# Four kinds of tiles at other places modulo 512 bytes, and the third group's values of two head pairs as one product of 512 columns

## The chip, the cores and the metric

The kernel runs on one core of a Trainium2 chip. The metric is device time in microseconds of one execution; less is better. A core has a matrix engine (TensorE, PE in the profile; its loading of the operand that stays in the array is listed apart as PEld), VectorE (DVE), ScalarE (ACT), GpSimd (POOL) and SyncE (SP, which issues DMAs here). They run side by side and wait for each other through semaphores; each works through its own instructions in the order in which the program has them.

## The reference

Four residual layers over x of 256 tokens by 1024 features, `x = x + mixer(rms_norm(x))`, with the mixers A, B, C, A. Each mixer is one input projection that also makes a gate z, some mixing, a product with silu(z), and an output projection.

```python
def mixer_a(h, w_in, v_gain, w_s, b_s, w_out):      # layers 0 and 3
    u, v, z = split(h @ w_in)                       # 2048 columns each
    mixed = einsum('gij,bcjgd->bcigd', tril(w_s), rms_norm(v, v_gain)) + b_s
    return (u * mixed * silu(z)) @ w_out

def mixer_b(h, w_in, q_gain, k_gain, w_out):        # layer 1: 8 heads of 128, three groups g
    for g, (window, dilation) in enumerate(((128, 1), (512, 4), (2048, 16))):
        q, k = rotary(rms_norm(q_g)), rotary(rms_norm(k_g))
        o_g, lse_g = banded_softmax_attention(q, k, v_g)
    return (sum_g softmax(lse)_g * o_g * silu(z)) @ w_out

def mixer_c(h, w_in, w_grp, scale, w_out):          # layer 2: four pooling groups g
    mixed_g = (causal_mean(x_g, window_g) - x_g) @ w_grp[g]
    return (mixed * scale * silu(z)) @ w_out
```

## The kernel before

**Products.** Every fp32 number that enters a large product is split in two tiles, an upper half (name ending in h, written by ScalarE, `hi_of`, line 85) and the remainder (ending in l, written by VectorE, `lo_of`, line 88). `mm3` (lines 80 to 82) then makes a product of three matrix instructions: upper by upper, upper by lower, lower by upper. In `mm3(out, lh, rh)` the tile lh is loaded into the array and rh streams past; the profile prints the streaming one first where names are told apart.

**Weights** come as 272 units of 128 by 1024 (`wts`, made on the host by `_weight_stream`). SP loads a unit into a raw tile wr (4 buffers); ScalarE and VectorE make w<n>h and w<n>l of it (7 pairs). `step` keeps that work a few units ahead of the product: the order in which these halves stand between an engine's other instructions is fixed when the program is built.

**Order.** The program is written by one Python loop that emits the projections. Side work stands in generators (`spawn`), and each `tick`, one per half unit of products, lets those that are due emit their next piece. `need(key)` ticks until a side task has emitted what the next product reads. So all five engines' orders are fixed, and how much work of TensorE stands between two steps of a side chain (its cover) comes from how many ticks lie between them.

**Projections.** `proj_tok` makes a product by tokens: h^T is loaded (tile hT, layout 128 by 8 by 256 per half) and 512 columns of weights stream; a unit takes 12 instructions. `proj_feat` makes it by features: weights are loaded and 256 columns of h^T stream; a unit takes 24. Both use PSUM banks of the tag pp (4 banks). Mixing uses the tag at (3 banks).

**Layer 1** (`layer_b`) runs over four head pairs hp of two heads. Of each it makes q and k of the three groups (qk, 4 units each), the values of the first two groups (v01, 4 units, 512 columns) and the values of the third (v2p, lines 1010 to 1019: 2 units, 256 columns). The gate (bz, two `proj_feat`) stands after the first qk. Side chains: `qk_task` (norm, rotation, transposes qt), `score_task` for each of two heads (scores s, maximum with the mask, exp into p, division by the sum), and `mix_task` (lines 909 to 976): five chunks, each of transposes pt of p, halves pT<hp><chunk>h and l, and products onto the tile o. A step of its loop emits the transposes of chunk i, the lower half of chunk i-1 and the products of chunk i-2. Then `gated` multiplies o with the gate (szT) and makes the halves yb<hp>. `proj_out` follows: units w144 to w147 for the first two pairs, w148 and w149 for the third (yb2), w150 and w151 for the fourth (yb3); the last four run for tokens 0 to 127 and then again for 128 to 255.

**Places.** hT holds two halves and 16 spare columns, and `h_parts` (line 267) shifts its start by 64 bytes in some layers. Odd widths of small tiles (32 in place of 16 for csc, line 1034) move the tiles behind them.

Of the kernel before, what the change touches and what calls it, by code (L numbers as in the profile page):

```python
# [10 lines left out]
F32 = mybir.dt.float32  # L11
# [6 lines left out]
P = 128  # L18
# [32 lines left out]
def hybrid_trunk_kernel(ctx, tc, x, wts, norm_gainT, a_v_gain, a_wsT, a_bsT, b_gl, b_gv, c_scaleT,  # L51
# [7 lines left out]
    dp = ctx.enter_context(tc.tile_pool(name="dp", bufs=1, space=bass.MemoryType.DRAM))  # L59

# [23 lines left out]
    def hi_of(hi, src):  # L84
        nc.scalar.activation(hi, src, AF.Copy)
# [66 lines left out]
    last_pool = [None]  # L152
# [10 lines left out]
    def load_units(n):  # L163
        while loaded[0] < min(n, n_seq):
            i = loaded[0]
            tag = raw_place(i)
            pool = {"wr": wp, "xs": cp, "wx": last_pool[0]}[tag]
            raw = pool.tile([P, 2, HALF], F32, tag=tag, name=f"wr{i}", bufs=len(raw_users[tag]))
            raw_users[tag] = raw_users[tag][1:] + [i]
            src = sums[seq[i][0], seq[i][2]][seq[i][1]] if isinstance(seq[i], tuple) else wts[seq[i]]  # L170
            nc.sync.dma_start(raw, src.rearrange("p (k n) -> p k n", n=HALF))
            raws.append(raw)
            loaded[0] += 1

    def sums_of_quarters(parts):
# [3 lines left out]
        for n, j, c in parts:  # L179
            z = seven_units(n) + j  # L180
            cs = slice(c * 256, (c + 1) * 256)
            q = cp.tile([P, 4, 256], F32, tag="xs", name=f"qs{n}{j}{c}", bufs=1)
# [84 lines left out]
    def h_parts(layer):  # L267

        o = 16 if layer in (0, DEPTH - 1) else 0
        return [hT[:, o + i * KT * S:o + (i + 1) * KT * S].rearrange("p (k s) -> p k s", s=S) for i in range(2)]  # L270
# [271 lines left out]
    def layer_a(layer, consts, pl, mid):  # L542
        hcur[:] = h_parts(layer)
        last_pool[0] = pl
# [10 lines left out]
        def v_task(n, o):  # L555
# [31 lines left out]
            for t in range(2):  # L587
                yield 1
                wh, wl = pair(pl, [P, 8, P], "wsr", f"wsr{layer}{t}", 2)
# [194 lines left out]
    def layer_b(layer, consts, pl):  # L784
# [124 lines left out]
        def mix_task(hp, vals, szT):  # L909
            vh, vl, v2h, v2l = vals  # L910

            def val(g, t, h):
# [3 lines left out]
                sl = slice(h * HD, (h + 1) * HD)  # L916
# [44 lines left out]
            for i in range(nch + 2):  # L961
                if i >= 2:
                    while ("v", hp) not in done or ("v2", hp) not in done:
                        yield 1
                    product(i - 2)
# [12 lines left out]
        def val_task(hp, o, vh, vl):  # L978
# [5 lines left out]
            done.add(("v", hp))  # L984

        def val2_task(hp, vp, v2h, v2l):
            fl = "p t c -> p (t c)"
            hi_of(v2h.rearrange(fl), vp)
            yield 1
            lo_of(v2l.rearrange(fl), vp, v2h.rearrange(fl))  # L990
            done.add(("v2", hp))
# [8 lines left out]
        for hp in range(NHEAD // 2):  # L1000
# [6 lines left out]
            o = proj_tok(f"v01{hp}")  # L1007
            vh, vl = pair(pl, [P, 2, HALF], "v01", f"v01{hp}", 1)
            spawn(val_task(hp, o, vh, vl))
            vp = pp(f"v2p{hp}")  # L1010
            for j in range(2):
                w = [a.rearrange("p a b -> p (a b)") for a in next_unit()]
                for kk in range(4):
                    k = 4 * j + kk
                    ws = [a[:, kk * 256:(kk + 1) * 256] for a in w]
                    for t in range(2):
                        mm3(vp[:, t * 256:(t + 1) * 256], h_t(k, t), ws, k == 0 and t == 0, k == KT - 1)
                    if kk % 2:
                        step(kk // 2)
            v2h, v2l = pair(pl, [P, 2, 256], "v2", f"v2{hp}", 1)  # L1020
            spawn(val2_task(hp, vp, v2h, v2l))
# [10 lines left out]
    def layer_c(layer, pl):  # L1032
        hcur[:] = h_parts(layer)
        csc = pl.tile([P, 32], F32, name="csc")[:, :16]
# [83 lines left out]
        def group_task(g, o):  # L1118
            yh, yl = pair(pl, [P, 4, S], "cy", f"cy{g}", 4)
# [82 lines left out]
def _weight_stream(a_w_in, a_w_out, b_w_in, b_w_out, c_w_in, c_w_grp, c_w_out):  # L1202
# [13 lines left out]
    for hp in range(4):  # L1216
        def cols(kind, g):
            c = kind * 3072 + g * 1024 + hp * 256
            return w[:, c:c + 256]
# [6 lines left out]
        parts.append(cols(2, 2).reshape(2, 4, P, 256).transpose(0, 2, 1, 3).reshape(2, P, UNIT))  # L1226
# [86 lines left out]
```

## Time and profile before

| | us |
|---|---|
| median of three runs | 836.82 (833.32, 837.32, 836.82) |
| the profiled execution, whole | 833.59 |
| its span, first to last instruction | 831.8 |
| stretch of layer 0 / 1 / 2 / 3 in it | 0 to 189 / 189 to 491 / 491 to 620 / 620 to 831.8 |

How such a profile is read. The page gives busy time by engine and the chain of work that ended last, followed back from the end. The list of waits says who waited for whom. The timeline has one instruction in a row: its start in us from the span's start, its duration in us, the engine, the line of the source, the operation, output and inputs by name, the shape, and in square brackets the engine's idle time before it with what ended it. Instructions of TensorE are pipelined: a product of 512 columns is shown with 0.39 us, but the next one starts 0.23 us later. What one more product costs is therefore read from the distance of two starts, not from the duration.

### The profile page before, as it was taken

How to read it: one execution, taken by the hardware profiler on the slowest of the kernel's cores; microseconds unless marked ns; L12 is line 12 of the kernel's file. 1: busy time of each engine (PE TensorE's matmuls, PEld its weight loads, DVE VectorE, ACT ScalarE, POOL GpSimd, SP SyncE). 2: the span in 40 equal slices, each digit the busy share in tenths (PEclk: the TensorE clock that was granted, in tenths of full speed). 3: DMA queues.
4: the chain of work that ended last, by engine and by line, in shares of the span. 5: the costliest groups of instructions: out<-in, count | busy, mean ns of one | idle time of the engine just before them, and what ended most of it. 6: DMA issues, size and time to landing. Idle time of an engine off the chain costs nothing.

```text
span 831.8 us, 12513 instructions
## 1 busy us (share of the span) xinstructions
PE 825.4 (99%) x4565; PEld 713.8 (86%) x4565; DVE 590.5 (71%) x1006; ACT 507.3 (61%) x937; POOL 42.6 (5%) x69
## 2 busy tenths in 40 slices
PE   8999999999999999999999999999999999999998
PEld 7888888888988888888888889999978888888886
DVE  4777657646857678678678577798864798787951
ACT  6765454336768687688688567446553667555740
POOL 0201000000000010010010012000000000000000
PEclk9999999999999999999999999999999999999999
DMA  7878666652867546556555268767675377685831
GB/s 272 284 262 276 236 204 203 217 191 82 260 237 229 176 145 236 178 168 212 178 156 199 77 212 277 236 194 230 235 264 180 102 261 240 200 327 167 323 127 51
DMA packets 60654, 172.66 MB, mean 208 GB/s; under 512 B 5584, under 2 KB 22496, under 8 KB 60464
## 3 DMA queue, kind: packets, MB, share of 16 engines
q1 hardware_dynamic: 59328, 167.79, 60.7%
q0 software_dynamic: 976, 3.79, 1.5%
q8 instruction: 36, 0.59, 0.3%
q10 hardware_dynamic: 288, 0.28, 0.1%
q14 instruction: 26, 0.21, 0.1%
HBM read 162.40 MB, written 9.44 MB: 207 GB/s over the span
## 4 chain that ended last, share of the span: by engine, by line
PE 89%; DVE 5%; DMA 3%; issue 1%; ACT 1%; SPq 0%; ACTq 0%; DVEq 0%
PE wo L80 6%; PE wo L82 6%; PE wo L81 6%; PE qk L82 5%; PE qk L80 5%; PE qk L81 5%; PE v L80 5%; PE v L82 5%; PE v L81 5%; PE z L82 3%; PE z L80 3%; PE u L80 3%; PE u L81 3%; PE z L81 3%; PE u L82 3%; PE qt L832 1%
## 5 line engine op out<-in xcount | busy, mean ns | idle before, releaser
L807 POOL TENSOR_TENSOR qr<-qm,m 128x8 f32<-128x8 f32 x12 | 19.9, 1660 | 228.3 <-DVE qm L806 228.3
L802 ACT ACTIVATE junk<-qk 128x128 bf16<-128x128 f32 x96 | 26.7, 278 | 7.3 <-PE qk L82 4.6
L811 ACT ACTIVATE qn<-qk,qr 128x128 f32<-128x128 f32 x96 | 27.6, 382 | 3.5 <-POOL qr L807 3.5
L186 DVE TENSOR_TENSOR qs<-qs 128x256 f32<-128x256 f32 x64 | 26.9, 420 | 3.8 <-DMA qs<-in_wts_dram 3.3
L512 DVE TENSOR_TENSOR x<-wo,x 128x512 f32<-128x512 f32 x16 | 11.0, 690 | 20.1 <-PE wo L82 20.0
L308 ACT ACTIVATE hT<-hp,gT 128x128 fp32r<-128x128 f32 x48 | 13.1, 383 | 14.9 <-PE hp L304 14.9
L806 DVE TENSOR_SCALAR qm<-qs 128x8 f32<-128x8 f32 x12 | 2.1, 172 | 23.7 <-ACT junk L802 23.7
L802 ACT ACTIVATION_READ_ACCUMULATOR junk<-qk 128x1 f32 x96 | 18.8, 196 | 0.0
L313 DVE SCALAR_TENSOR_TENSOR hT<-hp,gT,hT 128x128 fp32r<-128x128 f32 x48 | 13.5, 344 | 7.4 <-ACT hT L308 7.4
L290 POOL TENSOR_TENSOR r<-ms,m 128x1 f32<-128x1 f32 x6 | 4.3, 710 | 273.6 <-DVE ms L287 273.6
L282 ACT ACTIVATE junk<-x 128x512 bf16<-128x512 f32 x16 | 10.2, 640 | 9.6 <-DVE x L512 9.4
L901 ACT ACTIVATE p<-p,rl 128x384 f32<-128x384 f32 (+1 forms) x16 | 11.5, 769 | 5.0 <-DVE rl L900 5.0
L624 DVE SCALAR_TENSOR_TENSOR sz<-u,m,sz 128x512 f32<-128x512 f32 x8 | 6.0, 746 | 12.1 <-PE u L82 12.1
L832 PE MATMUL qt<-ident,qn 128*128 128x128 f32 x96 | 14.4, 273 | 0.1
L832 PEld LDWEIGHTS qt<-ident,qn 128*128 128x128 f32 x96 | 11.5, 140 | 3.0 <-issue 0.7
L824 DVE TENSOR_TENSOR rb<-qn,kcb 128x32 f32<-128x32 f32 x96 | 13.8, 184 | 0.0
L562 DVE TENSOR_TENSOR vv<-v,kc 128x512 f32<-128x512 f32 x16 | 10.7, 687 | 4.1 <-ACT junk L560 3.7
L897 ACT ACTIVATE p<-p,nb 128x768 f32<-128x768 f32 x8 | 7.5, 938 | 7.3 <-DVE nb L896 7.3
L820 DVE TENSOR_TENSOR ra<-qn,kcb 128x64 f32<-128x64 f32 x48 | 10.6, 221 | 0.8 <-ACT qn L811 0.2
L629 DVE SCALAR_TENSOR_TENSOR yy<-mx,bs,sz 128x256 f32<-128x256 f32 x24 | 10.5, 480 | 0.4
L391 DVE SCALAR_TENSOR_TENSOR hT<-hp,gT,hT 128x256 fp32r<-128x256 f32 x8 | 3.5, 476 | 9.4 <-ACT hT L387 9.4
L932 PE MATMUL pt<-ident,p 128*128 128x128 f32 x48 | 9.9, 274 | 0.0
(2887 smaller groups left out, 3314.3 us busy)
## 6 DMA issues: line engine op xcount, KB each, us to landing
wr<-in_wts_dram SPq DMA_DIRECT2D x267, 512.0 KB, 4.3
qs<-in_wts_dram SPq DMA_DIRECT2D x16, 512.0 KB, 5.0
sums<-qs SPq DMA_DIRECT2D x16, 512.0 KB, 6.2
wr<-sums SPq DMA_DIRECT2D x16, 512.0 KB, 4.4
kc<-in_a_wsT_dram POOLq DMA_DIRECT2D x2, 512.0 KB, 7.2
kc<-in_a_v_gain_dram POOLq DMA_DIRECT2D x1, 1024.0 KB, 5.0
out_dram<-x SPq DMA_DIRECT2D x4, 256.0 KB, 2.0
kc<-in_a_v_gain_dram POOLq DMA_DIRECT2D x1, 768.0 KB, 6.0
```

What stands on the lines that cost most here:

```text
L80: nc.tensor.matmul(out_ap, lh[0], rh[0], start=start, stop=False, skip_group_check=True)
L81: nc.tensor.matmul(out_ap, lh[0], rh[1], start=False, stop=False, skip_group_check=True)
L82: nc.tensor.matmul(out_ap, lh[1], rh[0], start=False, stop=stop, skip_group_check=True)
L186: nc.vector.tensor_tensor(q[:, a], q[:, a], q[:, b], op=ALU.add)
L308: nc.scalar.activation(h_parts(layer)[0][:, k, t * P:(t + 1) * P], pt[:, k % 4], AF.Copy, scale=gT[:, layer, k:k + 1])
L313: nc.vector.scalar_tensor_tensor(hTl, pt[:, k % 4], gT[:, layer, k:k + 1], hTh.bitcast(F32), op0=ALU.mult, op1=ALU.subtract)
L802: nc.scalar.activation(junk[:, :HD], ov[t][:, h], AF.Square, accum_out=ssq[t][:, h:h + 1])
L807: nc.gpsimd.tensor_tensor(rqs, ms, m05_row[:, :8], op=ALU.pow)
L811: nc.scalar.activation(qn[t][:, h], ov[t][:, h], AF.Copy, scale=rq[t][:, h:h + 1])
L824: nc.vector.tensor_tensor(rb[:, hs, s0:s0 + 16], qn[t][:, hs, s1:s1 + 16], c, op=ALU.mult)
L832: nc.tensor.transpose(pts[t][:, h], qn[t][:, h], ident)
L901: nc.scalar.activation(f, f, AF.Copy, scale=rl[i][:, 0:1])
```

## The change

Five tiles or groups of tiles start at other places. The places follow from the sizes of the tiles allocated before them; as the built programs lay them out, modulo 512 bytes:

| tile | role in the product | before | after |
|---|---|---|---|
| w..h, w..l (weights) | streams or is loaded | 384 | 384 |
| hT in layers 0 and 3 | loaded | 384 | 384 |
| hT in layer 1 | loaded in qk, v01, v2; streams in bz | 320 | 384 |
| hT in layer 2 | streams in cx, cz; loaded in the first cz | 320 | 320 |
| cd (differences, product cg of layer 2) | streams | 256 | 320 |
| wsr (w_s rows times the norm, product mx) | loaded | 384 | 192 |
| v01 (values, product o) | loaded | 384 | 192 |
| v2 (third group's values, product o) | loaded | 384 | 384 |
| cy (layer 2's y, product wo) | loaded | 384 | 128 |
| pT, qk, yb, v and y of layers 0 and 3 | either | 384 | 384 |

The third group's values are made for two head pairs at once, after the even pair's v01: `proj_tok` with 512 columns, 4 units; the odd pairs make none. The host orders their weights so, and the units keep their number. The upper half of these values goes to the tile xs of the pool cp, which the norms use too. The tiles stage (for the quarter sums of layer 3's weights, which shared xs before) and wx (a raw weight tile of layer 3's) now are tiles of their own from the start. The scratch for the descriptors of the DMAs that POOL issues is 8192 bytes in place of 16384.

```diff
+    stage = cp.tile([P, 4, 256], F32, name="stage")
+    wx = cp.tile([P, 2, HALF], F32, name="wx")
...
-            pool = {"wr": wp, "xs": cp, "wx": last_pool[0]}[tag]
-            raw = pool.tile([P, 2, HALF], F32, tag=tag, name=f"wr{i}", bufs=len(raw_users[tag]))
+            raw = wx if tag == "wx" else (wp if tag == "wr" else cp).tile(
+                [P, 2, HALF], F32, tag=tag, name=f"wr{i}", bufs=len(raw_users[tag]))
...
-            q = cp.tile([P, 4, 256], F32, tag="xs", name=f"qs{n}{j}{c}", bufs=1)
+            q = stage
...
-        o = 16 if layer in (0, DEPTH - 1) else 0
+        o = 0 if layer == 2 else 16
...
+                if t == 0:
+                    pl.tile([P, 80], F32, name="gap")
                 wh, wl = pair(pl, [P, 8, P], "wsr", f"wsr{layer}{t}", 2)
...
-                sl = slice(h * HD, (h + 1) * HD)
+                sl = slice(hp % 2 * 256 + h * HD, hp % 2 * 256 + (h + 1) * HD)
                 return v2h[:, t, sl], v2l[:, t, sl]
...
-                    while ("v", hp) not in done or ("v2", hp) not in done:
+                    while ("v", hp) not in done or ("v2", hp - hp % 2) not in done:
...
             o = proj_tok(f"v01{hp}")
+            if hp == 0:
+                pl.tile([P, 80], F32, name="gap1")
             vh, vl = pair(pl, [P, 2, HALF], "v01", f"v01{hp}", 1)
-            spawn(val_task(hp, o, vh, vl))
-            vp = pp(f"v2p{hp}")
-            for j in range(2):
...
-                        mm3(vp[:, t * 256:(t + 1) * 256], h_t(k, t), ws, k == 0 and t == 0, k == KT - 1)
...
-            v2h, v2l = pair(pl, [P, 2, 256], "v2", f"v2{hp}", 1)
-            spawn(val2_task(hp, vp, v2h, v2l))
+            if hp == 0:
+                pl.tile([P, 48], F32, name="gap2")
+            spawn(val_task(("v", hp), o, vh, vl))
+            if hp % 2 == 0:
+
+                v2h = cp.tile([P, 2, HALF], F32R, tag="xs", name=f"v2{hp}h", bufs=1)
+                v2l = pl.tile([P, 2, HALF], F32R, tag="v2l", name=f"v2{hp}l", bufs=1)
+                spawn(val_task(("v2", hp), proj_tok(f"v2{hp}"), v2h, v2l))
             spawn(mix_task(hp, (vh, vl, v2h, v2l), szT[:, hp]), LAST_LAG if hp == NHEAD // 2 - 1 else MIX_LAG)
...
-        csc = pl.tile([P, 32], F32, name="csc")[:, :16]
+        csc = pl.tile([P, 48], F32, name="csc")[:, :16]
...
+            if not yT:
+                pl.tile([P, 48], F32, name="gap")
             yh, yl = pair(pl, [P, 4, S], "cy", f"cy{g}", 4)
...
-        parts.append(cols(2, 2).reshape(2, 4, P, 256).transpose(0, 2, 1, 3).reshape(2, P, UNIT))
+        if hp % 2 == 0:
+            parts.append(_units(np.concatenate([cols(2, 2), cols(2, 2, 1)], axis=1)))
...
-    nc = _bacc.Bacc("TRN2", target_bir_lowering=False, num_devices=1)
+    nc = _bacc.Bacc("TRN2", target_bir_lowering=False, num_devices=1,
+                     dynamic_dma_scratch_size=8192)
```

How the engines' orders move, at three places. TensorE at the first head pair's values, where v01's last product ends; before, the third group's values of this pair alone (v2p, 256 columns):

```order
L80 MATMUL v_1_2361<-w87h,hT 128x512
L81 MATMUL v_1_2361<-w87l,hT 128x512
L82 MATMUL v_1_2361<-w87h,hT 128x512
L80 MATMUL v2p_2487<-w88h,hT 128x256
L81 MATMUL v2p_2487<-w88l,hT 128x256
L82 MATMUL v2p_2487<-w88h,hT 128x256
```

and after, where v_0_2487 is the third group's product for two pairs:

```order
L84 MATMUL v_1_2358<-w87h,hT 128x512
L85 MATMUL v_1_2358<-w87l,hT 128x512
L86 MATMUL v_1_2358<-w87h,hT 128x512
L84 MATMUL v_0_2487<-w88h,hT 128x512
L85 MATMUL v_0_2487<-w88l,hT 128x512
L86 MATMUL v_0_2487<-w88h,hT 128x512
```

The product of 512 columns has moved in from the second pair. Next, TensorE at the end of layer 1, in the last pair's mixing: o is the mixing's output, pt the transposes of the probabilities p, wo the output projection. Before:

```order
L82 MATMUL o_4845<-pT30h,v013l 128x256
L932 MATMUL pt_4921<-ident,p_4754 128x128
L930 MATMUL pt_4921<-ident,p_4823 128x128
L932 MATMUL pt_4921<-ident,p_4824 128x128 x2
L80 MATMUL wo_00_4809<-w146h,yb1h 128x512
L81 MATMUL wo_00_4809<-w146l,yb1h 128x512
L82 MATMUL wo_00_4809<-w146h,yb1l 128x512
L80 MATMUL wo_10_4811<-w146h,yb1h 128x512
L81 MATMUL wo_10_4811<-w146l,yb1h 128x512
L82 MATMUL wo_10_4811<-w146h,yb1l 128x512
L80 MATMUL o_4845<-pT31h,v23h 128x256
```

and after:

```order
L86 MATMUL o_4676<-pT30h,v013l 128x256
L936 MATMUL pt_4864<-ident,p_4694 128x128
L934 MATMUL pt_4864<-ident,p_4744 128x128
L936 MATMUL pt_4864<-ident,p_4745 128x128 x2
L84 MATMUL o_4676<-pT31h,v22h 128x256
L85 MATMUL o_4676<-pT31l,v22h 128x256
L86 MATMUL o_4676<-pT31h,v22l 128x256
```

The half unit of wo between the third transposes and the products on pT31 now stands earlier, beside the scores; the two later chunks have lost theirs too. Last, VectorE at the same end: w<n>l are weights' lower halves, rl the reciprocals of the second head's sums, szT the gating. Before:

```order
L88 TENSOR_TENSOR pT30l<-pt_4882,pT30h 128x512
L900 RECIPROCAL rl_4832<-l_4830 128x1
L900 RECIPROCAL rl_4833<-l_4831 128x1
L88 TENSOR_TENSOR pT31l<-pt_4896,pT31h 128x512
L88 TENSOR_TENSOR pT32l<-pt_4921,pT32h 128x512
L88 TENSOR_TENSOR w149l<-wr_4666,w149h 128x1024
L88 TENSOR_TENSOR pT33l<-pt_4948,pT33h 128x512
```

and after:

```order
L900 TENSOR_SCALAR nb_4750<-mx_4748 128x1
L92 TENSOR_TENSOR w150l<-wr_4597,w150h 128x1024
L92 TENSOR_TENSOR w151l<-wr_4624,w151h 128x1024
L92 TENSOR_TENSOR pT30l<-pt_4814,pT30h 128x512
L904 RECIPROCAL rl_4753<-l_4751 128x1
L904 RECIPROCAL rl_4754<-l_4752 128x1
L92 TENSOR_TENSOR pT31l<-pt_4839,pT31h 128x512
L92 TENSOR_TENSOR pT32l<-pt_4864,pT32h 128x512
```

The lower halves of the last two output units, which stood behind the first gating, now stand ahead of pT30l and the reciprocals.

More of the change, by code (lines that the diff above doesn't have):

```diff
@@ L151, in hybrid_trunk_kernel @@
     raw_users = {"wr": [-1] * RAW_BUFS, "xs": [-1], "wx": [-1]}
-    last_pool = [None]
     def raw_place(i):
@@ L543, in layer_a @@
         hcur[:] = h_parts(layer)
-        last_pool[0] = pl
         first = proj_first(f"v{layer}0") if layer == 0 else None
@@ L976, in mix_task, with val_task @@
             done.add(("yb", hp))
-        def val_task(hp, o, vh, vl):
+        def val_task(key, o, vh, vl):
             for t in range(2):
@@ L983, in val_task @@
                 lo_of(vl[:, t], o[t], vh[:, t])
[L984 to L991, printed above, removed]
+            done.add(key)
         def gate(b):
@@ L1007, in layer_b @@
             o = proj_tok(f"v01{hp}")
+            if hp == 0:
+                pl.tile([P, 80], F32, name="gap1")
             vh, vl = pair(pl, [P, 2, HALF], "v01", f"v01{hp}", 1)
-            spawn(val_task(hp, o, vh, vl))
-            vp = pp(f"v2p{hp}")
-            for j in range(2):
[L1012 to L1016, printed above, removed]
-                        mm3(vp[:, t * 256:(t + 1) * 256], h_t(k, t), ws, k == 0 and t == 0, k == KT - 1)
-                    if kk % 2:
-                        step(kk // 2)
-            v2h, v2l = pair(pl, [P, 2, 256], "v2", f"v2{hp}", 1)
-            spawn(val2_task(hp, vp, v2h, v2l))
+            if hp == 0:
[5 more added lines that the diff above has]
+                spawn(val_task(("v2", hp), proj_tok(f"v2{hp}"), v2h, v2l))
             spawn(mix_task(hp, (vh, vl, v2h, v2l), szT[:, hp]), LAST_LAG if hp == NHEAD // 2 - 1 else MIX_LAG)
@@ L1216, in _weight_stream, with cols @@
     for hp in range(4):
-        def cols(kind, g):
-            c = kind * 3072 + g * 1024 + hp * 256
+        def cols(kind, g, after=0):
+            c = kind * 3072 + g * 1024 + (hp + after) * 256
             return w[:, c:c + 256]
```

## The prediction

> **What bounds the kernel now.** I read the page first, for the share of each engine and the chain that ended last.
>
> ```profile
> span 831.8 us, 12513 instructions
> ...
> PE 825.4 (99%) x4565; PEld 713.8 (86%) x4565; DVE 590.5 (71%) x1006; ACT 507.3 (61%) x937; POOL 42.6 (5%) x69
> ...
> PE 89%; DVE 5%; DMA 3%; issue 1%; ACT 1%; SPq 0%; ACTq 0%; DVEq 0%
> ```
>
> TensorE is busy for 99% of the span and carries 89% of the chain. The second view is the list of TensorE's waits, which is complete with three rows:
>
> ```profile
> PE warm L276 <- POOL m L258: 1.4, 1, 1.4
> PE hp L380 <- DMA x<-in_x_dram: 0.8, 2, 0.5
> PE wo L80 <- DVE cyy L1126: 0.2, 1, 0.2
> ```
>
> All its waits that the view lists come to 2.4 us, and 2.2 of them lie before the first product. So a change can win only by making TensorE's own stream shorter, and it can lose by giving TensorE something to wait for. A busy PE is modelled, so the third view is the timeline: the distance between the *starts* of products, which I call the pitch, tells what a product really costs.
>
> **Places and pitch.** The rows below are starts, each the first of a weight unit or a run; the count between two rows is the program's. "Place" is a tile's start modulo 512 bytes, from the table ahead.
>
> ```profile
> 526.23 0.28 PE L80 MATMUL cx<-hT,w164h 128*128 128x256 f32 x1
> ...
> 528.95 0.28 PE L80 MATMUL cx<-hT,w165h 128*128 128x256 f32 x1
> ...
> 567.45 0.28 PE L80 MATMUL cg<-cd2h,w179h 128*128 128x256 f32 x1
> ...
> 570.30 0.28 PE L80 MATMUL cx<-hT,w180h 128*128 128x256 f32 x1
> ...
> 70.21 0.28 PE L80 MATMUL mx<-v00h,wsr00h 128*128 128x256 f32 x1
> ...
> 71.64 0.40 PE L80 MATMUL u<-w22h,hT 128*128 128x512 f32 x1
> ...
> 209.67 0.28 PE L80 MATMUL bz<-hT,w69h 128*128 128x256 f32 x1
> ...
> 212.39 0.28 PE L80 MATMUL bz<-hT,w70h 128*128 128x256 f32 x1
> ...
> 470.19 0.28 PE L80 MATMUL o<-pT30h,v013h 128*128 128x256 f32 x1
> ...
> 470.90 0.27 PE L932 MATMUL pt<-ident,p 128*128 128x128 f32 x1
> ```
>
> - cx: 24 products of 256 columns in 2.72 us, 113.3 ns each. Moving operand h^T at 320, weights loaded at 384. bz, the gate of the second layer, stands the same way and has the same 113.3.
> - cg: 24 in 2.85 us, 118.75 ns. The same shape and the same weights, but the moving differences stand at 256.
> - mx: 12 in 1.43 us, 119.2 ns; both operands at 384. o: 6 in 0.71 us, 118.3 ns; both at 384.
>
> So a 256 column product is 5 to 6 ns dearer in three of the four pairs of places that occur, and only 320 against 384 is free. For 512 columns:
>
> ```profile
> 43.01 0.39 PE L80 MATMUL v<-w12h,hT 128*128 128x512 f32 x1
> ...
> 45.73 0.39 PE L80 MATMUL v<-w13h,hT 128*128 128x512 f32 x1
> ...
> 434.41 0.39 PE L80 MATMUL qk<-w136h,hT 128*128 128x512 f32 x1
> ...
> 437.16 0.39 PE L80 MATMUL qk<-w137h,hT 128*128 128x512 f32 x1
> ```
>
> In the first layer, with h^T (here the loaded operand) at 384, 12 products take 2.72 us, 226.7 ns each; in the second, with h^T at 320, 2.75 us, 229.2 ns.
>
> The Trainium skill speaks against all of this: its page "SBUF — State Buffer", section "SBUF: two separate sides", says that only the port pair shared by VectorE and GpSimd contends and that "PE, ACT, and DVE's dedicated pair never wait on anyone". By that rule the places cost nothing, and the sum would be +1.7 (rival 2) where the rows give -1.7; cx and cg, 113.3 and 118.75 with the same shape, disagree with it.
>
> **The change, part by part.**
>
> *h^T of the second layer from 320 to 384.* 576 products of qk and 192 of v01 load it. 768 x 2.5 ns = **-1.9 us**. The same move makes bz (192 products, h^T moving) a 384 against 384 pair, as mx is: 192 x (119.2 - 113.3) = **+1.1 us**. Both classes occur in the trace, so I take them whole; the ends are -1.2 for the first, if only part of the rows have the extra, and 0 for the second.
>
> *cg's differences from 256 to 320.* 192 products become the free pair: 192 x 5.45 ns = **-1.05 us**.
>
> *w_s rows and v01 from 384 to 192; the third layer's y (cy) from 384 to 128.* The trace has none of these pairs. For 256 columns the ends are 113.3 and 119.2; I take 113.3, because 192 lies 256 bytes, half a turn, from a distance of 448, the only one that is free. mx: 96 x 5.9 = **-0.57 us**, and 48 of o's 256 column products, 48 x 5 = **-0.2 us**. For cy, 190 products of 512 columns, the ends are 0 and 190 x 2.5 = +0.5; I take 0, since 128 lies half a turn from 384.
>
> *Third group's values.* Four times 48 products of 256 columns become two times 48 of 512.
>
> ```profile
> 452.25 0.28 PE L80 MATMUL v2p<-w142h,hT 128*128 128x256 f32 x1
> ...
> 453.67 0.60 PE L832 MATMUL qt<-ident,qn 128*128 128x128 f32 x4
> ...
> 455.47 0.28 PE L80 MATMUL v2p<-w143h,hT 128*128 128x256 f32 x1
> ...
> 456.83 0.22 PE L80 MATMUL s<-qk30h 128*128 128x128 f32 x1
> 456.89 0.28 PE L81 MATMUL s<-qk30l,qk30h 128*128 128x128 f32 x1
> ...
> 457.78 0.33 PE L80 MATMUL v2p<-w143h,hT 128*128 128x256 f32 x1
> ```
>
> One run of 12 has 1.42 us (118.3 ns), another 1.36 (113.3). 96 new ones at 226.7 are 21.8 us; 192 old ones are 21.8 to 22.7. I take 118 for most: **-0.8 us**, ends 0 and -0.95. Units, VectorE and ScalarE halves and evacuations stay as many.
>
> *What the move takes away: cover.* The last head pair no longer has its 48 v2p products (5.6 us) between its v01 and the output product. In the new order the output product's units w144 to w147 run while scores are made, and nothing but w148 and w149 for the first 128 tokens is left beside the transposes and products of the mixing, which stood between halves of w145 to w149. Its steps, from the trace:
>
> ```profile
> 464.09 0.28 PE L80 MATMUL s<-qk30h 128*128 128x256 f32 x1
> ...
> 465.15 0.40 PE L80 MATMUL wo<-w145h,yb0h 128*128 128x512 f32 x1
> ...
> 466.54 0.27 PE L930 MATMUL pt<-ident,p 128*128 128x128 f32 x1
> ...
> 466.90 0.47 PE L80 MATMUL wo<-w145h,yb0h 128*128 128x512 f32 x1
> ...
> 483.68 0.39 PE L80 MATMUL wo<-w151h,yb3h 128*128 128x512 f32 x1
> ```
>
> ```profile
> 466.56 0.94 ACT L897 ACTIVATE p<-p,nb 128x768 f32<-128x768 f32 x1 [0.87 <-DVE nb L896]
> ...
> 469.49 1.43 ACT L901 ACTIVATE p<-p,rl 128x384 f32<-128x384 f32 x2
> ...
> 474.35 0.60 ACT L85 ACTIVATE pT33h<-pt 128x512 fp32r<-128x512 f32 x1 [1.21 <-PE pt L932]
> ...
> 478.49 1.05 ACT L85 ACTIVATE w151h<-wr 128x1024 fp32r<-128x1024 f32 x1
> ...
> 481.52 0.42 ACT L85 ACTIVATE yb3h<-szT 128x256 fp32r<-128x256 f32 x1 [1.99 <-DVE szT L955]
> ```
>
> ```profile
> 468.10 0.69 DVE L88 TENSOR_TENSOR pT30l<-pt,pT30h 128x512 fp32r<-128x512 f32 x1 [1.58 <-ACT pT30h L85]
> 468.71 0.21 DVE L900 RECIPROCAL rl<-l 128x1 f32<-128x1 f32 x2
> ...
> 479.76 1.22 DVE L88 TENSOR_TENSOR w151l<-wr,w151h 128x1024 fp32r<-128x1024 f32 x1
> 481.06 0.43 DVE L955 TENSOR_TENSOR szT<-o,szT 128x256 f32<-128x256 f32 x1
> ```
>
> Count from the end of v013 (452.25 before). TensorE does 48 wo products (10.9), four transposes (0.36, as at 466.54) and scores (2 x 0.95, from 456.83; 2 x 1.06, from 464.09): the first pt issues at 15.3, and the last scores end at 12.5. The last exp starts 1.4 later, as at 465.15 to 466.56, and ends at 14.95. ScalarE then has w150h to 15.9, pT30h to 16.5, w151h to 17.5. VectorE's next row is w151l, to 18.7, and pT30l, the reciprocals and through them the two scalings on ScalarE all stand behind it: 19.4, 19.6, 21.0. The third pt needs those scalings; then pT32h 22.1, pT32l 22.8, and the products on pT32, pT33, pT34 to about 25.5, since each waits a little for its lower half; szT and yb3h make 26.5, and the second half of w150 ends at 27.3. TensorE's own work to that point is 15.3 + 1.6 (18 transposes) + 4.1 (36 mixing products) + 2.7 (w148, w149) + 1.4 (w150) = 25.1, so it waits 2.2 us. The stretch before took 483.68 - 452.25 = 31.4, or 25.8 without v2p's 5.6. Net **+1.7 us**; the ends are +0.2 (TensorE's own work alone, and the small delays stay) and +3.5.
>
> *At nothing:* the scratch for descriptors halves; its queue carries a dozen loads, issued early in a layer for users late in it, and no wait of TensorE ends on one. The quarter sums have a tile of their own and SP's order is unchanged. v2's upper half shares xs with the norms, whose next user, the third layer's norm, follows the last mixing product by several us. If that cover were gone, TensorE would wait for the difference; the trace shows none to size it by, and the upper end below holds it. The odd pairs' mixing starts sooner after v01, but between products of the next pair, so it stays covered.
>
> **Sum:** -1.9 + 1.1 - 1.05 - 0.57 - 0.2 - 0.8 + 1.7 = **-1.7 us**. The profiled execution took 833.59 (span 831.8 and 1.8 around it), so 831.9; the median of the three runs is 836.82, 0.4% above it, and the same difference gives 835.1.
>
> **Rivals.**
> 1. *The end of the second layer stays covered.* If w151's halves land before the last exp, VectorE is free and only the own work counts: +0.2 in place of +1.7, 833.6. Against it: in the order they stand ahead of pT30l. Chance 0.20.
> 2. *Places do nothing.* cx and cg would differ for another reason; every term of places falls, v2 with them, and the +1.7 remains: 838.5. Chance 0.07.
> 3. *Slower: the mixing's five chunks do not overlap.* o holds one of three banks and pt has two; if a chunk waits for the whole of the one before, each takes 0.36 + 0.25 + 0.60 + 0.69 + 0.8 = 2.7 us, 13.5 for five, and with the lowering of w151 (2.2) and the scalings (1.4) the chain from the first pt to the last product on pT34 is 17.1 instead of 10.2. Then +1.7 becomes +8.6, and the sum +5.2: 842.0. The kernel is slower than before from a chain of 11.9, a chunk's period of 1.7. Against it: before, pt31 was transposed while pT30 was lowered. Chance 0.08.
> 4. *Faster: the 128 column mixing products lose a wait too.* Of the nine products of a score the first came at 60 ns (456.83 to 456.89) and the other eight at 111 (0.89 us to 457.78). If the place is what holds those, two in three of the mixing's 48 on v01, now at 192, save 32 x 50 = 1.6 us, and with a free bz and a covered end the sum is -5.9: 830.9. Against it: every such run in the trace has the 111. Chance 0.15.
>
> The forecast itself, the sum within 1.5 us, has 0.50.
>
> **Numbers.** 0.5% is about what a measurement of this kernel can tell from no change; faster means under 832.6, slower over 841.0. Rival 4 and a little of rival 1 are faster, 0.20; rival 3 and the spread of runs are slower, 0.09; the rest, 0.71, is within. The range from 831.0 to 839.5 takes in the ends of the terms (-4.4 and +2.9) and the runs' own spread.
>
> **What would show it.** After: cg's unit in 2.72 us; qk's unit in 2.72; bz's unit up to 2.86; mx's run of 12 in 1.36 if 192 is free. From the last v013 product to the first w151 product 27.3 us, with gaps on TensorE before o<-pT30l and the third pt. A bz at 2.72, or a gapless mixing, would make the forecast too slow; a mixing chain over 12 us would make the kernel slower than before.

## The result and the profile after

| | us |
|---|---|
| before, median of 10 runs | 833.68 (831.44 to 837.32) |
| after, median of 10 runs | 839.51 (838.14 to 840.14) |
| after to before | 1.0063, 95% interval 1.0047 to 1.0079 |
| span of the profiled execution, before and after | 831.8, 838.4 |

The change makes the kernel slower by 0.6%. The forecast was 835.1 with a range up to 839.5, and no difference that can be measured. It stood on a median of three runs, 836.82, that ten runs put at 833.68; taken from its own sum, it said -1.7 us where the two profiled executions differ by +6.6. That 839.51 comes out beside the upper end of the range is owed to this base, 3.1 us too high, and not to the sum.

The page after has the same shape; its first line of engines and its chain:

```profile
span 838.4 us, 12307 instructions
...
PE 829.1 (99%) x4469; PEld 712.5 (85%) x4469; DVE 590.5 (70%) x1006; ACT 508.2 (61%) x937; POOL 45.6 (5%) x69
...
PE 86%; DVE 5%; DMA 3%; ACT 3%; issue 1%; POOL 0%; SPq 0%; DVEq 0%; ACTq 0%
```

TensorE is still busy for 99%, with 96 instructions fewer and 3.7 us more busy time. So part of the loss is no wait at all, but dearer products. The rest is in the list of TensorE's waits, which had three rows before:

```profile
PE warm L279 <- POOL m L261: 1.4, 1, 1.4
PE pt L936 <- ACT p L905: 1.0, 2, 0.5
PE pt L934 <- ACT p L905: 0.7, 1, 0.7
PE hp L383 <- DMA x<-in_x_dram: 0.7, 2, 0.4
PE o L84 <- ACT pT34h L89: 0.4, 1, 0.4
PE hp L307 <- DVE xs L301: 0.4, 1, 0.4
PE wo L84 <- DVE cyy L1122: 0.3, 1, 0.3
PE wo L84 <- ACT yb3h L89: 0.2, 1, 0.2
PE qt L836 <- DVE qk22l L844: 0.2, 1, 0.2
PE o L85 <- DVE pT30l L92: 0.2, 1, 0.2
```

The waits for m, for x and for cyy were there before. The new rows lie in the mixing of pair 1 (two of the three waits before pt), before the next pair's transposes qt, and at the end of layer 1 with the transposes hp behind it. The list gives the idle time of each wait and not all that it costs, so I also timed stretches: from the start of the first product on one unit to the same of a later unit, in the timelines. Before, the gate (w69 to w76) takes 19.97 us, the rest of layer 1 (w76 to w152) 262.01, layer 2's products (w152 to w192) 111.87, and its end (w192 to w200) 22.42. The differences from that, for every kernel of this study:

| kernel | gate | rest of layer 1 | layer 2 | its end | median us | ratio to before, interval |
|---|---|---|---|---|---|---|
| after | +1.05 | +3.45 | +2.53 | +0.01 | 839.51 | 1.0063 (1.0047, 1.0079) |
| e1 layer 2's places back | +1.05 | +3.48 | -0.01 | +1.12 | 837.58 | 1.0044 (1.0027, 1.0061) |
| e2 cd alone back | +1.05 | +3.48 | +1.51 | +0.10 | 838.54 | 1.0053 (1.0033, 1.0073) |
| e3 values apart | +1.05 | +0.10 | +2.53 | -0.62 | 835.76 | 1.0020 (1.0007, 1.0033) |
| e4 before, values merged | 0.00 | +3.99 | -0.01 | +0.49 | 837.38 | 1.0045 (1.0031, 1.0058) |
| e5 before, cd at 320 | +0.16 | -0.03 | -1.14 | +3.79 | 835.33 | 1.0021 (1.0003, 1.0038) |
| e6 layer 1's h^T back | 0.00 | +3.99 | +2.53 | -0.62 | 838.15 | 1.0064 (1.0047, 1.0081) |
| e7 halves of w earlier | +1.05 | +2.03 | +2.53 | -0.44 | 838.05 | 1.0058 (1.0040, 1.0075) |
| e8 pair 1 mixes later | +1.05 | +3.47 | +2.53 | -0.43 | 838.18 | 1.0067 (1.0051, 1.0083) |
| e9 all three back | 0.00 | +0.05 | -0.01 | -0.61 | 832.75 | 0.9984 (0.9968, 1.0000) |
| e10 before, cd at 320, sum moved | 0.00 | -0.01 | -1.14 | -0.65 | 831.20 | 0.9955 (0.9939, 0.9971) |
| e11 gains together | 0.00 | +0.04 | -1.15 | -0.65 | 829.92 | 0.9951 (0.9933, 0.9970) |
| e12 czs at 384 | +1.05 | +3.55 | -1.12 | +1.41 | 837.92 | 1.0044 (1.0027, 1.0061) |
| e13 squares later | +1.05 | +4.15 | +2.51 | +0.51 | 840.19 | 1.0082 (1.0067, 1.0096) |
| e14 mixing two ticks later | +1.05 | +3.13 | +2.53 | +0.92 | 839.58 | 1.0074 (1.0058, 1.0091) |
| e15 merged, waits mended | 0.00 | +3.12 | -1.14 | -0.65 | 834.02 | 1.0004 (0.9991, 1.0018) |

The stretch ahead of w69 differs by up to 2.7 us between the profiled executions, with the landing of the first loads; the four columns leave it out. They repeat to 0.1 or 0.2 us where the program is the same, apart from the end of layer 2, and tell more than the medians, whose intervals reach 1.1 to 1.7 us to either side.

**Layer 2 became slower in products that the change did not touch.** The view by stretches (microseconds, busy time and count of each engine, TensorE's granted clock as a share of full speed, DMA share, GB/s) has the 288 products of the first three cx and then the first 48 of cg; before:

```profile
515.35:547.99 32.64, 32.64 (x291) 32.64 (x290) 26.70 (x41) 16.34 (x21) 0.38 (x3) 1.00 0.64 210
547.99:553.69 5.70, 5.70 (x51) 5.70 (x49) 5.60 (x10) 2.31 (x5) 0.12 (x1) 1.00 0.87 272
```

and after:

```profile
519.85:553.77 33.92, 33.92 (x290) 33.92 (x289) 27.04 (x43) 16.61 (x21) 0.38 (x3) 1.00 0.63 202
553.77:559.43 5.66, 5.66 (x51) 5.66 (x49) 5.56 (x10) 2.56 (x4) 0.13 (x1) 1.00 0.82 271
```

cx went from 113.3 ns a product (32.64 / 288) to 117.8 (33.92 / 288) at a granted clock of 1.00, though h^T and the weights stand at the places where they stood. cg, which was to win 5.45 ns, won 0.8 (5.70 to 5.66 in 48). The timeline after shows where the dearer pitch begins:

```profile
507.79 0.28 PE L84 MATMUL cz<-hT,w156h 128*128 128x256 f32 x1
...
510.53 0.60 PE L1054 MATMUL czt<-ident,czs 128*128 128x128 f32 x4
510.88 0.37 PE L84 MATMUL cz<-hT,w157h 128*128 128x256 f32 x1
...
511.32 0.28 PE L84 MATMUL cz<-hT,w157h 128*128 128x256 f32 x1
...
512.23 0.28 PE L86 MATMUL cz<-hT,w157l 128*128 128x256 f32 x1
512.35 0.60 PE L1054 MATMUL czt<-ident,czs 128*128 128x128 f32 x4
512.70 0.36 PE L84 MATMUL cz<-hT,w157h 128*128 128x256 f32 x1
```

The 24 products from 507.79 still take 2.74 us up to the transposes. Behind the first four transposes eight distances take 0.91 us (511.32 to 512.23), 113.8 ns each. Behind the second four, from 512.70 on, every run of cz, cx and cg is at 117.8 until layer 2 ends. So something stays behind those second transposes. The wider csc had moved not only cd but also czs, the tile that they load, from 256 to 320: the table of places in the change's section did not list it.

### The profile page after: what moved, and what is told of

Read it like the earlier page. It is cut to its first block, busy times and chain, and to the rows that moved or that the text cites. A ratio compares the mean times of both kernels' runs of the same rounds, so it can differ in the third digit from the quotient of the medians.

```text
span 838.4 us, 12307 instructions
## 1 busy us (share of the span) xinstructions
PE 829.1 (99%) x4469; PEld 712.5 (85%) x4469; DVE 590.5 (70%) x1006; ACT 508.2 (61%) x937; POOL 45.6 (5%) x69
## 3 DMA queue, kind: packets, MB, share of 16 engines
q0 software_dynamic: 976, 3.79, 1.3%
## 4 chain that ended last, share of the span: by engine, by line
PE 86%; DVE 5%; DMA 3%; ACT 3%; issue 1%; POOL 0%; SPq 0%; DVEq 0%; ACTq 0%
PE wo L84 5%; PE wo L86 5%; PE wo L85 5%; PE v L84 5%; PE v L85 5%; PE v L86 5%; PE qk L84 5%; PE qk L86 5%; PE qk L85 5%; PE z L86 3%; PE u L84 3%; PE z L84 3%; PE u L85 3%; PE u L86 3%; PE z L85 3%; PE cx L85 1%
## 5 line engine op out<-in xcount | busy, mean ns | idle before, releaser
L189 DVE TENSOR_TENSOR stage<-stage 128x256 f32<-128x256 f32 x64 | 26.9, 420 | 2.4 <-DMA stage<-in_wts_dram 1.9
```

The lines of the kernel that those rows point to most:

```text
L189: nc.vector.tensor_tensor(q[:, a], q[:, a], q[:, b], op=ALU.add)
```

## Experiments

**e1 and e2, which of layer 2's tiles.** e1 puts both back, e2 only cd; the first diff is that of e1.

```diff
-        csc = pl.tile([P, 48], F32, name="csc")[:, :16]
+        csc = pl.tile([P, 32], F32, name="csc")[:, :16]
...
-                pl.tile([P, 48], F32, name="gap")
+                pl.tile([P, 64], F32, name="gap")
```

And e2:

```diff
             w = POOLS[g]
+            if not dT:
+                pl.tile([P, 112], F32, name="gapd")
             dh, dl = pair(pl, [P, 4, S], "cd", f"cd{g}", 2)
...
-                pl.tile([P, 48], F32, name="gap")
+                pl.tile([P, 64], F32, name="gap")
```

> The changed kernel with layer 2's differences (cd) and everything behind them in that layer back at the place they had before (cd at 256, the gate's tiles czs and sz at 256 in place of 320); y (cy) stays at 128, layers 0, 1 and 3 as changed. Theory A (the products of cx and cz, whose operands and places did not change, lost their 113.3 ns because cg at 256 is what brought them back to it each time): cx and cz at 113.3 again, cg at 118.8, layer 2 shorter by 2.5 us, whole time about 837.0. Theory B (cx and cz are slow because of how layer 1 ended or because of what else moved, stage, wx and xs): cx and cz stay at 117.8, cg 118 to 119, whole time 839.5 to 839.7.

> The changed kernel with only the differences cd (and the tiles behind them) back at 256, while the gate's tiles czs and sz stay at 320, where the change put them; cy at 128. It parts the two tiles that the wider csc moved together. Theory A1 (cg's own place decides): as the run with both back, cx and cz at 113.3 after the first cg, about 837.0. Theory A2 (the transposes of czs at 320, after which the run at 117.8 began, decide): 117.8 for cx and cz throughout, about 839.5. Mixed: 117.8 until the first cg (288 products, +1.3 us) and 113.3 behind it, about 838.3.

e1: 837.58; layer 2 is back to 0.01 us. So its 2.5 us come from the places of layer 2 alone, not from how layer 1 ends. The median fell by 1.9 only, since the end of layer 2 took 1.1 more (TensorE waited 1.3 there for cyy). e2: 838.54; 117.8 from the transposes until the first cg, whose products at 256 cost 118.8, and 113.3 behind it: layer 2 at +1.51, where 1.3 was worked out. Both theories had a part: czs at 320 brings the dearer pitch, and cg at 256 ends it.

**e5 and e12, the same pair of places at both pitches.** e5 is the kernel before with cd at 320 but czs left at 256, and cy kept at 384:

```diff
+            if not dT:
+                pl.tile([P, 16], F32, name="gapd")
             dh, dl = pair(pl, [P, 4, S], "cd", f"cd{g}", 2)
...
+            if not yT:
+                pl.tile([P, 112], F32, name="gap")
             yh, yl = pair(pl, [P, 4, S], "cy", f"cy{g}", 4)
```

e12 is the changed kernel with czs at 384, and cd at 320 as changed:

```diff
-        csc = pl.tile([P, 48], F32, name="csc")[:, :16]
+        csc = pl.tile([P, 64], F32, name="csc")[:, :16]
...
+            if not dT:
+                pl.tile([P, 112], F32, name="gapd")
```

> The kernel before with one place altered: layer 2's differences cd at 320 (as changed), the gate's tiles czs and sz kept at 256, y (cy) kept at 384. Theory H (a run of 256 column products keeps the pitch that it has while its places stay 320 and 384; what comes ahead decides which of the two it is; the transposes of czs at 320 bring 117.8, those of czs at 256 leave 113.3): cx, cz and cg all at 113.3, layer 2 shorter by 192 x 5.45 ns = 1.05 us than before, 832.6. Rival (cd at 320 itself brings the pair to 117.8): cg at 117.8 and cx, cz behind the first cg at 117.8, that is 288 x 4.5 - 192 x 1 = +1.1 us, 834.8.

> The changed kernel with the gate's tiles czs and sz at 384 instead of 320; cd at 320 and cy at 128 as changed. Which places of the loaded czs bring the 117.8? Theory 1 (320 alone does, the place at which h^T streams behind it): cx, cz and cg at 113.3, 192 x 4.5 + 480 x 4.5 ns = 3.0 us less in layer 2, 836.5 to 837.5 with a wait before w193 as in the run with both places back. Theory 2 (256 alone leaves 113.3): 117.8 in all of layer 2, 839.5.

The products do what theory H and theory 1 say. The stretches of e5 at the same two places:

```profile
515.33:547.97 32.64, 32.64 (x290) 32.64 (x289) 26.36 (x41) 16.33 (x21) 0.37 (x3) 1.00 0.62 207
547.97:553.41 5.44, 5.44 (x50) 5.44 (x49) 5.34 (x10) 2.04 (x5) 0.12 (x1) 1.00 0.87 282
```

cg now has 113.3 ns (5.44 / 48), the gain that the forecast promised; e12's layer 2 is as short (-1.12) with cd in the same place in which the change left it. So 320 against 384 runs at 113.3 or at 117.8 for as long as no other place comes between, and what ran ahead decides: behind the transposes of czs stand 117.8 when czs is at 320, and 113.3 when it is at 256 or 384. The gate's other tile, sz, moves with czs, but no instruction of TensorE reads it. The place alone is not the whole rule: in the changed kernel and in all seven others with czs at 320 the first four transposes leave 113 to 114, and only the second four, from the same place, leave 117.8. Why, no run here shows.

But e5's time is 835.33 (830.48 to 838.34), not 832.6. Its end of layer 2 lost 3.8 us. The timeline of its VectorE and then of TensorE:

```profile
585.44 0.43 DVE L186 TENSOR_TENSOR qs<-qs 128x256 f32<-128x256 f32 x1 [1.61 <-DMA qs<-in_wts_dram]
...
601.82 1.23 DVE L88 TENSOR_TENSOR w195l<-wr,w195h 128x1024 fp32r<-128x1024 f32 x1 [1.70 <-ACT w195h L85]
605.74 1.23 DVE L88 TENSOR_TENSOR w196l<-wr,w196h 128x1024 fp32r<-128x1024 f32 x1 [2.70 <-ACT w196h L85]
```

```profile
607.80 0.64 PE L80 MATMUL wo<-w193h,cy3h 128*128 128x512 f32 x1 [2.54 <-DVE cyy L1130]
608.24 0.63 PE L81 MATMUL wo<-w193l,cy3h 128*128 128x512 f32 x1
608.67 0.63 PE L82 MATMUL wo<-w193h,cy3l 128*128 128x512 f32 x1
```

VectorE waits for the load of a quarter sum, everything behind that add is late, weights are lowered late and so loaded late, and cyy stands behind the last of them. e12 has the same wait of TensorE for cyy with 1.7 us. TensorE's wait for cyy was 0.2 us before: it is a second bound, just behind the first.

**e10, that bound taken away.** e5 with one quarter sum made in layer 0 instead of at the end of layer 2:

```diff
-PARTS = (4, 8)
+PARTS = (5, 8)
```

> The kernel before with cd at 320 (czs at 256, cy at 384), and one of the quarter sums made in layer 0 instead of at the end of layer 2 (PARTS 5 and 8 in place of 4 and 8, the last four sums become three). In the run with cd at 320 alone layer 2's products became 1.15 us shorter, and then TensorE waited 2.7 us for cyy and ran its next 12 products at twice their pitch; VectorE had waited 1.6 us for the load of the fourth sum and everything behind that add was late. Theory (that sum's load, 5.8 us, sets VectorE's order at the end of layer 2): wait before w193 gone, 832.2 (833.6 - 1.15 - 0.3). Rival (the raw weights' loads are late by themselves): the wait stays, 834 to 836.

831.20, ratio 0.9955: the wait is gone (end of layer 2 at -0.65), the chain that ended last is TensorE for 99%, and the 1.14 us of layer 2 arrive. e10 takes the sum's load and its add away together and no run moves the sum alone, so which of the two set the bound, and what the move would give by itself, is not shown.

**e3 and e4, the merged values.** e3 undoes the merging in the changed kernel, in the host's order of units too:

```diff
-            if hp % 2 == 0:
-
-                v2h = cp.tile([P, 2, HALF], F32R, tag="xs", name=f"v2{hp}h", bufs=1)
-                v2l = pl.tile([P, 2, HALF], F32R, tag="v2l", name=f"v2{hp}l", bufs=1)
-                spawn(val_task(("v2", hp), proj_tok(f"v2{hp}"), v2h, v2l))
+            vp = pp(f"v2p{hp}")
+            for j in range(2):
...
+            v2h, v2l = pair(pl, [P, 2, 256], "v2", f"v2{hp}", 1)
+            spawn(val2_task(hp, vp, v2h, v2l))
```

e4 keeps the merging and takes out the places: the four tiles named gap, gap1 and gap2, the wider csc, and the shift of h^T in layer 1.

> The changed kernel with the third group's values again made for each head pair by itself (256 columns, as before the change), all places as changed. Theory (the merged product takes cover away from the first pair's mixing, 1.7 us, and from the end of layer 1, 2.6 us, and saves 0.8 in the product itself): 3.5 us less, about 836.0; no wait of TensorE over 0.3 us at the end of layer 1. Rival (the cover is not what it costs, the places of layer 1 and the state of TensorE are): within 1 us of the changed kernel, 838.5 to 840.

> The kernel before with only the third group's values of two pairs made as one product (with the tiles of their own for the quarter sums and the raw weights that this needs, and the smaller scratch); all places modulo 512 as before, but xs and one raw tile from 352 to 384. Theory (merging costs 1.7 + 2.6 us of cover and saves 0.8 in the product): slower than before by 3.5 us, 837.2. Rival (the loss is in the places alone): 833 to 834, as before. Layer 2 is expected at 113.3 for cx and cz.

e3: 835.76. The rest of layer 1 stands at +0.10: with h^T at 384 the products of v2p come every 120.5 ns, not 118.4 as before, which eats what h^T brings elsewhere (e9, with h^T at 320, stands at +0.05). Its list of TensorE's waits has no row left in layer 1:

```profile
PE warm L279 <- POOL m L261: 1.4, 1, 1.4
PE hp L383 <- DMA x<-in_x_dram: 0.8, 2, 0.5
```

e4: 837.38, with the rest of layer 1 at +3.99. From both sides the merged product costs 3.7 us of time, 3.4 to 4.0 in the stretch, where the forecast had +0.9.

**e7, the end of layer 1.** The constant that says how many units ahead the output product of layer 1 has its halves made:

```diff
-LAST_AHEAD = 3
+LAST_AHEAD = 5
```

> The changed kernel with the halves of the output product's units of layer 1 made two units earlier (LAST_AHEAD 5 in place of 3), so that w150l and w151l no longer stand on VectorE between the last exp and pT30l, the reciprocals and the scalings. Theory (at the end of layer 1 the lowering of w150 and w151 in that chain sets the waits before pt<-p and o<-pT30l, some 1.1 of the 2.6 us): 1.2 us less, 838.3, those two waits gone, those before pT34 and yb3 left. Rival (the chain of the five chunks itself is what TensorE waits for): 0.3 us or less, 839.2 to 839.6, the wait only moves from the third pt to the later chunks.

The rest of layer 1 becomes 1.42 us shorter (3.45 to 2.03). The end's waits for p, pT30l and xs are gone; pT34h, 0.4, and yb3h, 0.2, are left; the two rows before pt that remain are pair 1's. The medians say 838.05 against 839.51, the ratios 1.0058 against 1.0063, too near to tell; the stretch decides. The lowering of w150 and w151 ahead of pT30l and the scalings, which the forecast named, is that part. In the timeline of the changed kernel it reads so, VectorE first:

```profile
475.57 1.23 DVE L92 TENSOR_TENSOR w150l<-wr,w150h 128x1024 fp32r<-128x1024 f32 x1 [2.05 <-ACT w150h L89]
477.11 1.23 DVE L92 TENSOR_TENSOR w151l<-wr,w151h 128x1024 fp32r<-128x1024 f32 x1 [0.32 <-ACT w151h L89]
478.25 0.68 DVE L92 TENSOR_TENSOR pT30l<-pt,pT30h 128x512 fp32r<-128x512 f32 x1
478.85 0.21 DVE L904 RECIPROCAL rl<-l 128x1 f32<-128x1 f32 x2
```

The last exp ends at 474.5; its reciprocal comes 4.4 us later, behind both halves. On TensorE, in the same timeline, the third pt waits for the scaling behind it:

```profile
479.80 0.31 PE L934 MATMUL pt<-ident,p 128*128 128x128 f32 x1
480.60 0.44 PE L936 MATMUL pt<-ident,p 128*128 128x128 f32 x2 [0.49 <-ACT p L905]
```

**e8, e13 and e14, pair 1's mixing.** e8 starts it 4 ticks later, e14 6 (the same line with 6):

```diff
-... LAST_LAG if hp == NHEAD // 2 - 1 else MIX_LAG)
+... LAST_LAG if hp == NHEAD // 2 - 1 else MIX_LAG + 4 * (hp % 2))
```

e13 makes one piece of ScalarE's work later:

```diff
+            if (hp, g) == (2, 0):
+                yield 3
             square(0)
             square(1)
```

> The changed kernel with the mixing of the odd head pairs but the last (pair 1) started 8 ticks after v01 in place of 4, the length of the 2 units that no longer stand there. Theory (pair 1's two waits of 0.9 and 0.8 us before pt<-p are lost cover and nothing else): 1.7 us less, 837.8, both waits gone. Rival (the wait comes back elsewhere, since the mixing then falls between the next pair's q and k with their own chains): 839.0 to 839.6.

e8 failed as an experiment: the first transposes wait for p, and with 4 ticks or 8 they come to stand at the same place; the waits stayed. It tells nothing about lost cover. ScalarE in the changed kernel, between the exp and the scaling, the first and the last of the 16 squares:

```profile
346.69 0.94 ACT L901 ACTIVATE p<-p,nb 128x768 f32<-128x768 f32 x1
...
349.17 0.27 ACT L806 ACTIVATE junk<-qk 128x128 bf16<-128x128 f32 x1
...
352.14 0.20 ACT L806 ACTIVATION_READ_ACCUMULATOR junk<-qk 128x1 f32 x1
...
352.71 1.44 ACT L905 ACTIVATE p<-p,rl 128x384 f32<-128x384 f32 x2
```

The scaling starts 6 us after its exp started, behind the squares of the next pair's first q and k; before, it started 3.4 after (341.12 and 344.52 in that timeline) and ahead of the squares. The odd pair has no v2p any more, so the next pair's q and k end two units sooner, and the squares have overtaken the scaling. On TensorE two transposes of pair 1's third chunk then wait:

```profile
352.39 0.27 PE L936 MATMUL pt<-ident,p 128*128 128x128 f32 x1
353.37 0.33 PE L934 MATMUL pt<-ident,p 128*128 128x128 f32 x1 [0.71 <-ACT p L905]
354.20 0.44 PE L936 MATMUL pt<-ident,p 128*128 128x128 f32 x2 [0.49 <-ACT p L905]
```

They start 0.98 and 0.83 after the one ahead of them, where 0.11 is usual: 1.6 us are lost.

> The changed kernel with the squares (and the norm behind them) of one product only, the third pair's first q and k (qk20), made 3 ticks later, so that on ScalarE they stand behind the scaling of pair 1's p instead of ahead of it; TensorE's order around it stays, except that qk20's transposes come 3 ticks later. Theory S (ScalarE's order: 16 squares, 3.2 us, ahead of the scaling): both waits of pt<-p near 352 us gone, 1.7 us less, 837.8. Theory C (the mixing of pair 1 lacks cover whatever ScalarE does): waits stay within 0.3 us, 839.2 to 839.6.

> The changed kernel with pair 1's mixing started 10 ticks after v01 in place of 4, which is 2 ticks (1 unit, 2.7 us) later than where it came to stand. Theory S and theory C both say that the two waits before pt<-p go, since 2.7 us of products come ahead of the third pt and the scaling stands behind the same squares: 837.8. If the mixing then falls among the next pair's transposes and their chain, the waits return there: 838.5 to 839.5.

e13: both waits near 352 us are gone, as theory S has it; the list shows what came in their place:

```profile
PE qt L836 <- DVE qk20l L844: 1.6, 1, 1.6
...
PE o L85 <- DVE pT14l L92: 0.5, 1, 0.5
```

The pair whose squares were put off is now late with its own transposes: from the first product on w112 to that on w116 it takes 1.3 us less than the changed kernel, from there to w120 2.0 more. The rest of layer 1 is 0.7 us longer than after the change, and the median is 840.19. e14 replaces the waits by one of 1.0 us before o<-pT10l, and the stretch gains 0.3; the medians, 839.58 and 839.51, show nothing. In three orders, then, this mixing finds no place that costs nothing.

**e6, layer 1's h^T** back at 320:

```diff
-        o = 0 if layer == 2 else 16
+        o = 16 if layer in (0, DEPTH - 1) else 0
```

> The changed kernel with the second layer's h^T back at 320 (as before), everything else as changed. Forecast's sizing: bz back to 113.3 saves 1.1 us, the 864 products that load h^T cost 2.5 ns each, +2.2: 840.6. Sizing by the means after the change (0.5 to 1 ns per product, since many rows at 232 and 236 stay): -1.1 + 0.6, 839.0. If bz now stands at 117.8 as layer 2 does: -0.4 + 0.6, 839.7.

The gate is free again (1.05), and the rest of layer 1 costs 0.54 more: of qk, v01 and v2 together 864 products, 0.6 ns each. The end of layer 2 gave 0.6 beside that. The median is 838.15 and the ratio 1.0064, so this net half microsecond is read from the stretches, not from the times.

**e9, e11 and e15, put together.** e9 undoes values, layer 2's places and h^T in one kernel; e11 is e9 with cd at 320 and the sum moved; e15 is e11 with the values merged, the squares later and `LAST_AHEAD` 5.

> The changed kernel with three parts undone together: values of the third group apart for each pair, layer 2's cd and czs back at 256, layer 1's h^T back at 320. What is left of the change: w_s rows and v01 at 192, y of layer 2 at 128, the quarter sums and the raw weights in tiles of their own, the smaller scratch. If the three costs add up as measured one by one (3.75, 1.9 and 1.35 us), 839.5 - 7.0 = 832.5, that is a little under before, of which the w_s rows explain 0.5 by their pitch (96 products, 119.4 to 117.8, and what the first layer's start differs). If something else in the change costs: 834 or more.

> As the run with all three parts undone, but with cd at 320 (czs at 256) and the sum moved to layer 0: what the experiments so far leave as gains, put together. Theory: 1.05 to 1.3 us under the run with all three parts undone, about 831.3. Rival (cd at 320 gains nothing once the end of layer 2 is another): the same as that run, 832.5.

> The run with the gains put together (values apart, 829.9), but with the third group's values merged, the squares of qk20 later and the halves of the output product's units earlier. If the merged product's own saving (0.7 us) outweighs what is left of its waits at the end of layer 1 (2.6 - 1.4 = 1.2 us): under 829.9; by the sum of the runs so far, 3.75 - 1.7 - 1.4 = 0.65 us over it, 830.6.

e9: 832.75, no new cost left. e11: 829.92, ratio 0.9951 (0.9933 to 0.9970), faster than both kernels. e15: 834.02, so merging costs 4.1 us there by the medians, 3.1 by the stretch; with the squares put off, which loses in e13 too, the waits were not mended, only moved.

## Why the prediction was wrong

The forecast's sum was -1.7 us, the profiled executions differ by +6.6. Its terms, against the stretches:

- **cg from 256 to 320, -1.05; measured +2.5 in layer 2.** This step failed, and it is the largest part of the miss, 3.6 us. It said "So a 256 column product is 5 to 6 ns dearer in three of the four pairs of places that occur, and only 320 against 384 is free", and took a pitch for a property of two addresses. e5, e12 and e2 show that 320 against 384 has two pitches, and that the place of czs, which the transposes ahead load, decides between them; by what mechanism stays open. The gain that was forecast exists, exactly (e5, e10: -1.14); the change lost it by moving czs along, a tile that my table did not follow because it takes part in 8 transposes only.
- **Third group's values with the end of layer 1, -0.8 + 1.7; measured +4.0 (e4).** The mechanism at the end of the layer was right, and its parts were named (w150 and w151 ahead of pT30l and the scalings: e7). Its size was not: from the first product on w144 (459.28) to the first on w151 (487.63) it took 28.4 us, not 27.3, as the later chunks wait for pT34h and yb3h too, and behind it the transposes hp of the next layer waited 0.4 for xs. The forecast's own figures also give 27.3 - 25.8 = 1.5 there, where it wrote 1.7. Most of the rest is the step "The odd pairs' mixing starts sooner after v01, but between products of the next pair, so it stays covered". It was costed at nothing with TensorE's products as the cover; the cover was there (12 products of qk between the transposes, as before), and ScalarE's order was not looked at. The two late transposes cost 1.6 us, and e13, with the squares behind the scaling, is free of both.
- **h^T at 384, -1.9; measured -0.54 (e6).** Right in sign; the size came from units of 12 products without side work, 2.72 against 2.75 us. After the change such a unit takes 2.72, but over all qk products that follow one another the mean only went from 229.9 to 229.0 ns, since many starts at 232 and 236 stay.
- **bz, +1.1; measured +1.05 over seven of its eight units.** Right: a unit takes 2.88 us, 120 ns a product.

```profile
212.30 0.28 PE L84 MATMUL bz<-hT,w70h 128*128 128x256 f32 x1
...
215.18 0.28 PE L84 MATMUL bz<-hT,w71h 128*128 128x256 f32 x1
```

- **w_s rows and v01 at 192, -0.57 and -0.2.** mx has 117.8 ns, not 113.3; layers 0 and 3 win 0.2 us each (w16 to w60, and w200 to the end). In the changed kernel the median of o is 118 as before, no gain. 192 is not free.
- **At nothing:** cy at 128, the scratch and the tiles of their own cost nothing that e9 would show. The same holds for xs, which moved too, from 352 to 384, and is not in the table.

The differences, 3.6 + 3.1 + 1.4 + 0.3, come to 8.4, against 8.3 us between forecast and trace.

Of the rivals, the first falls: w151l (477.11) does stand ahead of pT30l, and even e7, where it does not, takes 27.2 us from w144 to w151, 1.4 over the 25.8 before. The second falls with e1 and e2: places do something. The rule of the Trainium skill's page "SBUF — State Buffer", section "SBUF: two separate sides", that TensorE never waits on anyone is not enough to foretell these pitches. It would have given layer 2 no loss, where 2.5 us were measured; whether the reading of memory is what differs, no run shows. The third rival's chain was near: from the first pt (474.90) to the output product (485.71) 10.8 us, under the 11.9 from which it would have decided, so the chunks do overlap. The fourth falls too: in e9, with v01 at 192, 44 of 60 distances behind a 128 column product of the mixing are 109 to 114 ns, and 44 of 60 were 108 to 113 before. The kernel became slower mainly by two things that were not on the list, the lasting 117.8 of layer 2 and the squares ahead of pair 1's scaling.

## What to carry to other kernels

A pitch that is read off one place of a trace belongs to that place and to what ran ahead of it; before it is carried over, look for the same operands at another pitch, and list every tile that the same edit moves, the ones with few instructions too. Where a product is taken out of TensorE's stream, check the orders of the other engines at the place where later work closes up: an operation of the next stage can overtake the one that a chain waits for. Where the bound engine gets faster, the next wait stands just behind it (here 1.15 us won, 3.8 lost, until a load was moved), so a gain is to be looked for again at the end of the stage.

## What the runs showed of the hardware

- Products with equal shapes and operands, at equal places modulo 512 bytes, ran at 113.3 (e12) or at 117.8 ns (the changed kernel) for over 90 us on end, by what had run ahead, at a granted clock of 1.00.
- In these traces a wait costs TensorE more than the idle time that is listed: the third pt at the end of layer 1 had 0.49 us of idle, and its start came 0.80 after the one ahead of it, where transposes that don't wait follow at 0.11.
- After the wait of 2.54 us in e5 the products on w193 came 0.43 us apart instead of 0.23, and the stretches show the granted clock:

```profile
605.00:607.80 2.80, 0.27 (x2) 0.00 (x0) 2.06 (x4) 0.72 (x2) 0.00 (x0) 1.00 0.56 219
607.80:611.40 3.60, 3.60 (x9) 2.81 (x10) 3.26 (x6) 3.45 (x5) 0.00 (x0) 0.53 0.47 148
611.40:616.00 4.60, 4.60 (x22) 3.79 (x21) 3.42 (x3) 2.47 (x3) 0.00 (x0) 1.00 0.71 214
```

For 3.6 us it is 0.53, which adds some 1.7 us (0.47 of it) to a wait of 2.5; the wait of 1.66 us before the same product in e12 was followed by products 0.23 to 0.33 apart. The Trainium skill's page "TensorE: Matmul & The Clock Gate", section "Why this matters for your kernels", sets the point at idle gaps of about 3 us. Here a listed idle of 2.5 (2.9 between the two starts) was enough, and 1.7 was not; nothing between them was seen.
